# A convolution's closing addition moved, precedence for masks and evacuations, and three later steps in a two-block transformer kernel

## The chip, the cores and the metric

The kernel runs on one core of a Trainium2 chip. The metric is the device time of one execution in microseconds (us). A core has five engines with a queue of their own each: PE (TensorE, the matmuls), DVE (VectorE), ACT (ScalarE), POOL (GpSimd) and SP (SyncE, which here only issues DMAs). An engine works its queue in order, and waits for others by semaphores.

## The reference

512 tokens of 1024 channels pass through two blocks, all in float32. The change concerns the second, which has two layers (0 and 1). Each layer projects the normed input once and gives slices of it to four branches, whose outputs go through one output projection:

```python
def conformer_conv_branch(val, glu_gate, gate, dw_w, dw_b, ln_g, ln_b, pw_w, pw_b):
    h = val * jax.nn.sigmoid(glu_gate)
    h = causal_depthwise_conv(h, dw_w, dw_b)
    h = jax.nn.silu(layer_norm(h, ln_g, ln_b))
...
def hgrn2_branch(q, f_raw, v, gate, lb, norm_g):
    ...
        scores = jnp.einsum('bhtk,bhsk,bhtsk->bhts', qt, kt, decay)
        o_intra = jnp.einsum('bhts,bhsv->bhtv', scores, vt)
...
def mla_branch(cq, ckv, k_rope, gate, positions, qa_g, qb_w, kva_g, kvb_w):
    q = (rms_norm(cq, qa_g) @ qb_w).reshape(bsz, s, D_HEADS, D_NOPE + D_ROPE)
    ...
```

The convolution has 31 taps on 256 channels, hgrn2 works in chunks of 64 tokens, and the fourth branch is a state-space one (ssd). The first block is not touched.

## The kernel before

**Matmuls.** A float32 product is made of three matmuls of parts: high weights by high and by low input, low weights by high input (`mm3`, L466 to L468, 128x512 a piece; L1469, L1470 and L1474 likewise; with tokens on the partitions L1493, L1494 and L1491, 128x256 a piece). Each weight group is loaded by SP (L436, `wr`), copied on ACT to `wh` (L439) and to `wl` = -`wh` (L441), and POOL then issues a DMA that adds the weights to `wl` (L442, 512 KB). So ACT and POOL's DMA queue carry the weights beside all else.

**Tasks.** The program of a layer runs through its projections on PE in order, and after each calls `pump()`, which lets every open task, a Python generator, go on to its next `yield`: `hgrn_task` twice (tasks 0 and 1), `mla_kv`, `mla_q`, `conf_conv`, and so on. The order in which the program writes instructions is their priority; `high_priority(offset=400)` puts what is written inside 400 places ahead. A scheduler then fixes each engine's order from the priorities and from a timeline that it keeps itself. So a `yield` more moves a task's later instructions behind some of the projections, and the order on the engines need not follow the program.

**Buffers.** 70 SBUF tiles of 128 partitions ("units") are given out and taken back as a queue, oldest first. A unit that is given out again makes its writer wait for the last reader, which may be a DMA. PSUM has tags pj (3 buffers), sA (2), sB (2), so (1).

**The convolution** (`conf_conv`, L1505 to L1541). For each of two halves of the channels ("conv 0", "conv 1") the taps 0 to 21 run on DVE into `c` (L1523), a product and an addition in one. The other nine are products on ACT (L1517, L1519 and seven of L1529, named here by their columns, x488 to x482), and POOL adds the seven to two accumulators `e` and `e2` in turn with accumulating DMAs (L1530). One more DMA adds `e2` to `e` (L1534), and DVE adds `e` to `c` (L1539). The task steps by tap pairs (`TAPS` = 2).

**hgrn** (`hgrn_task`, L1772 on). The scores in a chunk come in levels 1, 4, 8, 16, 32: for each, `hgrn_level` makes factors (L1676 to L1685 for level 1; L1695, L1696, L1697, L1705, L1706 for the others, on DVE, POOL and ACT), PE makes the scores (L345 for level 1, L1746 for the others), and `copy_predicated` on DVE puts them through a mask into D (L1766 for level 1, the "finest masks"; L1750 for the others). Behind the levels come three transposes of K2 on PE, their evacuation `kt` on ACT (L1811) and the states' matmuls `pn` (L1817).

**MLA.** `mla_kv` (L2069 on) turns the rotary part of the keys by products and a sum (L2078, L2080), a step later PE transposes them into sB (L2085). `mla_proj` (L2104 on) makes the queries with `mm3` into pj, evacuated on ACT in halves (L2115); the rotary part by DVE (L2124, L2125); the keys likewise (L2134, L2135).

Of the kernel before, what the change touches and what calls it, by code (L numbers as in the profile page):

```python
# [18 lines left out]
S = 512  # L19
# [293 lines left out]
class Build:  # L313
# [1191 lines left out]
    def conf_conv(self, l, ths):  # L1505
        nc = self.nc
        V, G = nc.vector, nc.gpsimd
        for i in range(2):
            while ths[i] is None:
                yield  # L1510
            th, aw = ths[i], self.aw
            c, e = self.unit(F32, "cc"), self.unit(F32, "ce")
            e2 = self.unit(F32, "ce")
            V.tensor_scalar(out=c[:, :S], in0=th[:, :S], scalar1=aw[:, i, 30:31],
                            scalar2=self.v(f"awb{l}", i, i + 1), op0=ALU.mult, op1=ALU.add)
            n0 = 31 - self.POOL_TAPS
            nc.scalar.activation(out=e[:, n0:S], in_=th[:, :S - n0], func=AF.Copy, scale=aw[:, i, 30 - n0:31 - n0])  # L1517
            k = n0 + 1
            nc.scalar.activation(out=e2[:, k:S], in_=th[:, :S - k], func=AF.Copy, scale=aw[:, i, 30 - k:31 - k])  # L1519
            rest = list(range(n0 + 2, 31))  # L1520
            acc = [e, e2]
            for o in range(1, n0):
                V.scalar_tensor_tensor(out=c[:, o:S], in0=th[:, :S - o], scalar=aw[:, i, 30 - o:31 - o], in1=c[:, o:S],  # L1523
                                       op0=ALU.mult, op1=ALU.add)
                if o % self.TAPS == 0:
                    if rest:
                        k = rest.pop(0)
                        t = self.unit()
                        nc.scalar.activation(out=t[:, :S - k], in_=th[:, :S - k], func=AF.Copy, scale=aw[:, i, 30 - k:31 - k])  # L1529
                        nc.gpsimd.dma_start(out=acc[0][:, k:S], in_=t[:, :S - k], accum_op=ALU.add)  # L1530
                        acc.reverse()
                        self.free(t)
                    elif e2 is not None:
                        nc.gpsimd.dma_start(out=e[:, n0 + 1:S], in_=e2[:, n0 + 1:S], accum_op=ALU.add)  # L1534
                        self.free(e2)
                        e2 = None
                    yield
            assert not rest and e2 is None
            V.tensor_tensor(out=c[:, n0:S], in0=c[:, n0:S], in1=e[:, n0:S], op=ALU.add)  # L1539
            self.free(th, e)  # L1540
            self.cs[i] = c  # L1541

    TAPS = 2
    POOL_TAPS = 9
# [193 lines left out]
    def hgrn_score(self, D, X, li, m):  # L1738
# [24 lines left out]
                          rhs=c[sl, w * 128 + 64:w * 128 + 128], start=True, stop=True)  # L1763
        for hh in range(2):
            if m == 1:
                nc.vector.copy_predicated(out=self.v4(D[hh]), mask=self.msk[li].unsqueeze(1).to_broadcast([128, 4, 128]),  # L1766
                                          data=p[hh].rearrange("p (w t) -> p w t", w=4))
            else:
                nc.scalar.activation(out=self.v4(D[hh])[0:64, :, 64:128],
                                     in_=p[hh][:64, :256].rearrange("p (w t) -> p w t", w=4), func=AF.Copy)  # L1770

    def hgrn_task(self, l, i, q_, k_, b_):  # L1772
# [16 lines left out]
        for n in range(5):  # L1789
            if n < 2:  # L1790
                yield
            if n < 3:
                X[LV[n + 2]] = self.hgrn_level(q, k, b, LV[n + 2], Z[(n + 1) % NZ])
            elif n == 3:
                KE, QE, K2, Q2, e = self.hgrn_wide(q, k, b)
                self.free(q_, k_, b_)
            m = LV[n]
            self.hgrn_score(D, X[m], n if n > 1 else 1 - n, m)
            yield
            yield  # L1800
            self.free(X[m][0])
            if m == 1:
                self.free(X[m][1])
# [7 lines left out]
        nc.scalar.activation(out=kt[:, :384], in_=pt[:, :384], func=AF.Copy)  # L1811
        self.hgrn_score(D, (KE, QE), 0, 64)
        self.free(KE, QE, K2)
        yield
        pn = self.sA()
        for w in range(3):
# [252 lines left out]
    def mla_kv(self, l, m):  # L2069
# [10 lines left out]
        V.tensor_tensor(out=kr, in0=kr, in1=t, op=ALU.add)  # L2080
        self.tok_norm(m, 1, 128, 1.0 / 128)
        yield
        pk = self.sB()
        for j in range(4):
            nc.tensor.transpose(pk[:32, j * 128:j * 128 + 128], kr[:, j * 32:j * 32 + 32], self.ident)  # L2085
# [18 lines left out]
    def mla_proj(self, w0, w1):  # L2104
# [6 lines left out]
        for t in range(2):  # L2111
            p = self.pj()
            self.mm3(p, w0[0], w0[1], t * 128, 128, 2, xq, slice(0, S), kstep=256)
            for hh in range(2):
                nc.scalar.activation(out=qs[t * 2 + hh][:64, :S], in_=p[hh * 64:hh * 64 + 64], func=AF.Copy, scale=SC)  # L2115
            self.pump()
        pr = self.pj()
        self.mm3(pr, w1[0], w1[1], 0, 128, 2, xq, slice(0, S))
# [2 lines left out]
        for x in xq:  # L2121
            self.free(*x)
        ro, t = self.unit(), self.unit()
        V.tensor_tensor(out=ro[:, :S], in0=pr, in1=self.cosT, op=ALU.mult)  # L2124
        V.tensor_tensor(out=t[:, :S], in0=px, in1=self.sinT, op=ALU.mult)  # L2125
        G.tensor_tensor(out=ro[:, :S], in0=ro[:, :S], in1=t[:, :S], op=ALU.add)
        for h in range(4):
            nc.scalar.activation(out=qs[h][64:96, :S], in_=ro[h * 32:h * 32 + 32, :S], func=AF.Copy, scale=SC)
# [2 lines left out]
        for t in range(2):  # L2131
            p = self.pj()
            self.mm3(p, w1[0], w1[1], 512 + t * 128, 128, 1, [xk], slice(0, S))
            nc.scalar.activation(out=ks[t * 2][:64, :S], in_=p[0:64], func=AF.Copy)  # L2134
            nc.scalar.activation(out=ks[t * 2 + 1][:64, :S], in_=p[64:128], func=AF.Copy)  # L2135
        self.pump()
        vt = []
        for t in range(2):
# [409 lines left out]
```

## Time and profile before

| what | value |
|---|---|
| three runs | 1370.59, 1372.15, 1372.16 us (median 1372.15) |
| profiled execution, own time | 1370.83 us |
| its span, first to last instruction | 1368.9 us |
| mean granted clock of TensorE | 0.988 |
| busy: PE, DVE, ACT, POOL | 97%, 57%, 57%, 32% of the span |

The page of the profile gives each engine's busy time, the chain of work that ended last (followed back from the last instruction, at each step to what released it), and the costliest groups of instructions. The list of waits says for one engine what it stood still for; the timeline lists its instructions one by one, and the table by stretch gives busy times and the granted clock (1.00 is 2.4 GHz, 0.5 is 1.2 GHz). The instructions whose order the change alters run from about 813 us to the end, those of layer 1 from about 1090 us.

### The profile page before, as it was taken

What the parts mean: (1) busy time and instruction counts of PE and PEld (TensorE: products, weight loads), DVE (VectorE), ACT (ScalarE), POOL (GpSimd) and SP (SyncE); (2) the same over time, 40 slices, a digit from 0 to 9 for tenths busy, and PEclk for the clock granted to TensorE, in tenths of its full rate; (3) what the DMA queues carried; (4) which work ended last, traced back from release to release, by engine and by line L of the source; (5) the groups of instructions that cost most, each with busy time, mean ns of one, the idle gap of its engine ahead of it and who ended that gap; (6) DMA issues with size and microseconds to landing.
All of it is one profiled execution on the core that took longest, in us unless ns stands there. A gap on an engine that the chain in (4) does not pass through costs nothing.

```text
span 1368.9 us, 22975 instructions
## 1 busy us (share of the span) xinstructions
PE 1329.9 (97%) x8778; PEld 1195.9 (87%) x8778; DVE 783.2 (57%) x1961; ACT 782.3 (57%) x1218; POOL 439.1 (32%) x547
## 2 busy tenths in 40 slices
PE   8999999999999999999999999899999889999997
PEld 8888899999999988998898788788988888789986
DVE  8989775423524321332233395798732797987623
ACT  7656564754555443444444775675556876764653
POOL 4557632113332221221123462332211453422210
PEclk9999999999999999999999999999999999999999
DMA  8945566598888889888887975796467676893573
GB/s 269 253 96 109 121 127 138 123 222 186 187 189 186 189 186 188 189 186 190 189 180 150 220 164 131 149 203 136 100 133 166 133 170 138 181 211 81 119 151 92
DMA packets 76861, 223.49 MB, mean 163 GB/s; under 512 B 11216, under 2 KB 21968, under 8 KB 76752
## 3 DMA queue, kind: packets, MB, share of 16 engines
q0 software_dynamic: 32256, 106.53, 47.3%
q1 hardware_dynamic: 43488, 113.80, 25.2%
q8 instruction: 69, 1.13, 0.4%
q10 hardware_dynamic: 1008, 1.70, 0.3%
q14 instruction: 40, 0.33, 0.1%
HBM read 209.33 MB, written 4.72 MB: 156 GB/s over the span
## 4 chain that ended last, share of the span: by engine, by line
PE 77%; DVE 11%; DMA 5%; ACT 3%; issue 3%; POOL 1%; SPq 0%; DVEq 0%; POOLq 0%; ACTq 0%
PE pj L466 14%; PE pj L468 14%; PE pj L467 14%; PE pj L1469 3%; PE pj L1470 3%; PE pj L1474 3%; PE pj L1493 2%; PE pj L1494 2%; PE pj L1491 2%; PE sB L493 2%; DMA ce<-u 2%; DMA wl<-in_wst 2%; PE sB L2167 1%; PE so L2195 1%; DVE hZ L1705 1%
## 5 line engine op out<-in xcount | busy, mean ns | idle before, releaser
L466 PE MATMUL pj<-xh,wh 128*128 128x512 f32 (+4 forms) x1468 | 463.7, 316 | 6.5 <-ACT mq L2115 4.7
L467 PE MATMUL pj<-xl,wh 128*128 128x512 f32 (+4 forms) x1468 | 461.4, 314 | 0.0
L468 PE MATMUL pj<-xh,wl 128*128 128x512 f32 (+4 forms) x1468 | 460.7, 314 | 0.1
L439 ACT ACTIVATE wh<-wr 128x1024 fp32r<-128x1024 f32 (+2 forms) x197 | 204.0, 1036 | 325.0 <-PE pj L467 258.0
L442 POOL DMA_DIRECT2D wl<-in_wst x192 | 170.5, 888 | 568.7 <-ACT wl L441 540.6
L466 PEld LDWEIGHTS pj<-xh,wh 128*128 128x128 f32 x1468 | 278.1, 190 | 25.3 <-ACT mq L2115 4.8
L467 PEld LDWEIGHTS pj<-xl,wh 128*128 128x128 f32 x1468 | 278.1, 189 | 18.3 <-issue 0.6
L468 PEld LDWEIGHTS pj<-xh,wl 128*128 128x128 f32 x1468 | 278.1, 189 | 18.1 <-DMA wl<-in_wst 0.6
L441 ACT ACTIVATE wl<-wh 128x1024 fp32r<-128x1024 f32 (+2 forms) x192 | 198.9, 1036 | 16.4 <-PE pj L1474 8.9
L1494 PE MATMUL pj<-wh,xl 128*128 128x256 f32 x384 | 98.4, 292 | 0.0
L1493 PE MATMUL pj<-wh,xh 128*128 128x256 f32 x384 | 98.0, 291 | 0.0
L1469 PE MATMUL pj<-xh,wh 128*128 128x512 f32 x232 | 93.0, 401 | 0.0
L1470 PE MATMUL pj<-xl,wh 128*128 128x512 f32 x232 | 92.5, 399 | 0.0
L1493 PEld LDWEIGHTS pj<-wh,xh 128*128 128x128 f32 x384 | 74.1, 193 | 1.3 <-issue 1.0
L1494 PEld LDWEIGHTS pj<-wh,xl 128*128 128x128 f32 x384 | 74.3, 194 | 0.8 <-issue 0.5
L1407 DVE TENSOR_TENSOR hT<-hT,pj 128x512 f32<-128x512 f32 x24 | 16.4, 687 | 88.8 <-PE pj L468 88.8
L1523 DVE SCALAR_TENSOR_TENSOR cc<-u,aw,cc 128x511 f32<-128x511 f32 (+17 forms) x84 | 65.8, 786 | 0.6
L1474 PE MATMUL pj<-xh,wl 128*128 128x512 f32 x232 | 62.2, 400 | 0.0
L1386 DVE TENSOR_TENSOR u<-pj,nsR 128x258 f32<-128x258 f32 (+1 forms) x44 | 18.6, 425 | 75.6 <-PE pj L468 68.3
L1491 PE MATMUL pj<-wl,xh 128*128 128x256 f32 x384 | 57.1, 290 | 0.0
L1392 DVE TENSOR_TENSOR u<-u,pj 128x512 f32<-128x512 f32 x22 | 15.1, 687 | 64.6 <-PE pj L468 60.3
L1469 PEld LDWEIGHTS pj<-xh,wh 128*128 128x128 f32 x232 | 43.6, 188 | 9.3 <-issue 0.5
(636 smaller groups left out, 2550.9 us busy)
## 6 DMA issues: line engine op xcount, KB each, us to landing
wr<-in_wst SPq DMA_DIRECT2D x183, 512.0 KB, 4.1
wl<-in_wst POOLq DMA_DIRECT2D x180, 512.0 KB, 5.9
hT<-in_xT SPq DMA_DIRECT2D x16, 264.0 KB, 4.8
wr<-in_wst SPq DMA_DIRECT2D x8, 384.0 KB, 3.1
wl<-in_wst POOLq DMA_DIRECT2D x8, 384.0 KB, 5.7
wr<-in_wst SPq DMA_DIRECT2D x6, 256.0 KB, 2.7
UD<-us SPq DMA_DIRECT2D x4, 264.0 KB, 7.4
U<-UD SPq DMA_DIRECT2D x16, 66.0 KB, 5.0
```

Of the source, the lines that this page charges most:

```text
L439: nc.scalar.activation(out=h[:, c], in_=raw[:, c], func=AF.Copy)
L441: nc.scalar.activation(out=l[:, c], in_=h.bitcast(F32)[:, c], func=AF.Copy, scale=-1.0)
L442: nc.gpsimd.dma_start(out=l[:, c], in_=self.ap["wst"][i, :, c], accum_op=ALU.add)
L466: mm(out=out, lhsT=a, rhs=xh[:, sl], start=k == 0, stop=False)
L467: mm(out=out, lhsT=a, rhs=xl[:, sl], start=False, stop=False)
L468: mm(out=out, lhsT=b, rhs=xh[:, sl], start=False, stop=k == nk - 1)
L1469: mm(out=p, lhsT=a, rhs=xh[:, :S], start=k == 0, stop=False)
L1470: mm(out=p, lhsT=a, rhs=xl[:, :S], start=False, stop=False)
L1474: mm(out=p, lhsT=wl[:, k * 128:k * 128 + 128], rhs=xh[:, :S], start=False, stop=k == 7)
L1491: mm(out=o, lhsT=xh[:, sl], rhs=ws[q][1][:, c], start=False, stop=q + u + k == 5)
L1493: mm(out=o, lhsT=xh[:, sl], rhs=ws[q][0][:, c], start=q + u + k == 0, stop=False)
L1494: mm(out=o, lhsT=xl[:, sl], rhs=ws[q][0][:, c], start=False, stop=False)
```

## The change

Three things, all in the second block:

1. `conf_conv`: the closing addition of `e` to `c` gets a function, `close`; that of conv 0 is made at the third tap pair of conv 1, that of conv 1 two steps after its last. The DMA that adds `e2` to `e` is issued at the tenth tap pair in place of the eighth.
2. `high_priority(offset=400)` around the finest masks and around MLA's evacuations (queries, rotary products, keys).
3. One `yield` more ahead of three places: in layer 1 before the first hgrn level that the loop makes, before `pn`, and before the transposes in `mla_kv`.

```diff
@@ -1505,6 +1505,13 @@
     def conf_conv(self, l, ths):
         nc = self.nc
         V, G = nc.vector, nc.gpsimd
+        last = None
+
+        def close(i, c, e, n0):
+            V.tensor_tensor(out=c[:, n0:S], in0=c[:, n0:S], in1=e[:, n0:S], op=ALU.add)
+            self.free(e)
+            self.cs[i] = c
+
         for i in range(2):
             while ths[i] is None:
                 yield
@@ -1530,15 +1537,20 @@
                         nc.gpsimd.dma_start(out=acc[0][:, k:S], in_=t[:, :S - k], accum_op=ALU.add)
                         acc.reverse()
                         self.free(t)
-                    elif e2 is not None:
+                    elif o + self.TAPS >= n0:
                         nc.gpsimd.dma_start(out=e[:, n0 + 1:S], in_=e2[:, n0 + 1:S], accum_op=ALU.add)
                         self.free(e2)
                         e2 = None
+                    if last and o >= 3 * self.TAPS:
+                        close(*last)
+                        last = None
                     yield
             assert not rest and e2 is None
-            V.tensor_tensor(out=c[:, n0:S], in0=c[:, n0:S], in1=e[:, n0:S], op=ALU.add)
-            self.free(th, e)
-            self.cs[i] = c
+            self.free(th)
+            last = (i, c, e, n0)
+        yield
+        yield
+        close(*last)
 
     TAPS = 2
     POOL_TAPS = 9
@@ -1763,8 +1775,9 @@
                           rhs=c[sl, w * 128 + 64:w * 128 + 128], start=True, stop=True)
         for hh in range(2):
             if m == 1:
-                nc.vector.copy_predicated(out=self.v4(D[hh]), mask=self.msk[li].unsqueeze(1).to_broadcast([128, 4, 128]),
-                                          data=p[hh].rearrange("p (w t) -> p w t", w=4))
+                with self.tc.high_priority(offset=400):
+                    nc.vector.copy_predicated(out=self.v4(D[hh]), mask=self.msk[li].unsqueeze(1).to_broadcast([128, 4, 128]),
+                                              data=p[hh].rearrange("p (w t) -> p w t", w=4))
             else:
                 nc.scalar.activation(out=self.v4(D[hh])[0:64, :, 64:128],
                                      in_=p[hh][:64, :256].rearrange("p (w t) -> p w t", w=4), func=AF.Copy)
@@ -1788,6 +1801,8 @@
             G.memset(t[:, :S], 0.0)
         for n in range(5):
             if n < 2:
+                yield
+            if l and n == 0:
                 yield
             if n < 3:
                 X[LV[n + 2]] = self.hgrn_level(q, k, b, LV[n + 2], Z[(n + 1) % NZ])
@@ -1811,6 +1826,7 @@
         nc.scalar.activation(out=kt[:, :384], in_=pt[:, :384], func=AF.Copy)
         self.hgrn_score(D, (KE, QE), 0, 64)
         self.free(KE, QE, K2)
+        yield
         yield
         pn = self.sA()
         for w in range(3):
@@ -2080,6 +2096,7 @@
         V.tensor_tensor(out=kr, in0=kr, in1=t, op=ALU.add)
         self.tok_norm(m, 1, 128, 1.0 / 128)
         yield
+        yield
         pk = self.sB()
         for j in range(4):
             nc.tensor.transpose(pk[:32, j * 128:j * 128 + 128], kr[:, j * 32:j * 32 + 32], self.ident)
@@ -2112,7 +2129,8 @@
             p = self.pj()
             self.mm3(p, w0[0], w0[1], t * 128, 128, 2, xq, slice(0, S), kstep=256)
             for hh in range(2):
-                nc.scalar.activation(out=qs[t * 2 + hh][:64, :S], in_=p[hh * 64:hh * 64 + 64], func=AF.Copy, scale=SC)
+                with self.tc.high_priority(offset=400):
+                    nc.scalar.activation(out=qs[t * 2 + hh][:64, :S], in_=p[hh * 64:hh * 64 + 64], func=AF.Copy, scale=SC)
             self.pump()
         pr = self.pj()
         self.mm3(pr, w1[0], w1[1], 0, 128, 2, xq, slice(0, S))
@@ -2121,8 +2139,9 @@
         for x in xq:
             self.free(*x)
         ro, t = self.unit(), self.unit()
-        V.tensor_tensor(out=ro[:, :S], in0=pr, in1=self.cosT, op=ALU.mult)
-        V.tensor_tensor(out=t[:, :S], in0=px, in1=self.sinT, op=ALU.mult)
+        with self.tc.high_priority(offset=400):
+            V.tensor_tensor(out=ro[:, :S], in0=pr, in1=self.cosT, op=ALU.mult)
+            V.tensor_tensor(out=t[:, :S], in0=px, in1=self.sinT, op=ALU.mult)
         G.tensor_tensor(out=ro[:, :S], in0=ro[:, :S], in1=t[:, :S], op=ALU.add)
         for h in range(4):
             nc.scalar.activation(out=qs[h][64:96, :S], in_=ro[h * 32:h * 32 + 32, :S], func=AF.Copy, scale=SC)
@@ -2131,8 +2150,9 @@
         for t in range(2):
             p = self.pj()
             self.mm3(p, w1[0], w1[1], 512 + t * 128, 128, 1, [xk], slice(0, S))
-            nc.scalar.activation(out=ks[t * 2][:64, :S], in_=p[0:64], func=AF.Copy)
-            nc.scalar.activation(out=ks[t * 2 + 1][:64, :S], in_=p[64:128], func=AF.Copy)
+            with self.tc.high_priority(offset=400):
+                nc.scalar.activation(out=ks[t * 2][:64, :S], in_=p[0:64], func=AF.Copy)
+                nc.scalar.activation(out=ks[t * 2 + 1][:64, :S], in_=p[64:128], func=AF.Copy)
         self.pump()
         vt = []
         for t in range(2):
```

Nothing is added or left out: every engine has as many instructions as before, and SP's order is the same. Line numbers grow by 7 to 20 (L1529 is L1536 after the change, L1685 is L1697, L1746 is L1758, L1766 is L1779, L1811 is L1826, L1890 to L1900 are L1906 to L1916, L2115 is L2133). Three places follow; out<-in are the program's tiles.

DVE in layer 0, the rows that end with the finest masks (L1766, hD<-msk,sB) of hgrn task 0, before (L509 to L519 and L1896 to L1901 are small steps on vectors of the norms and of ssd):

```order
L515 TENSOR_SCALAR s_8748<-s_8745 128x4
L517 TENSOR_TENSOR s_8747<-s_8746 128x4
L518 TENSOR_TENSOR s_8747<-s_8747,s_8748 128x4
L519 SCALAR_TENSOR_TENSOR s_8746<-s_8747,s_8746 128x4
L1685 TENSOR_TENSOR u_9076<-u_9076,u_8499 128x512
L517 TENSOR_TENSOR s_8747<-s_8746 128x4
L1898 RECIPROCAL s_8705<-s_8705 128x16
L1766 COPY_PREDICATED hD_8600<-msk,sB_8780 128x512
L1766 COPY_PREDICATED hD_8599<-msk,sB_8779 128x512
```

and now:

```order
L518 TENSOR_TENSOR s_8747<-s_8747,s_8748 128x4
L519 SCALAR_TENSOR_TENSOR s_8746<-s_8747,s_8746 128x4
L517 TENSOR_TENSOR s_8747<-s_8746 128x4
L1914 RECIPROCAL s_8705<-s_8705 128x16
L518 TENSOR_TENSOR s_8747<-s_8747,s_8748 128x4
L1915 TENSOR_TENSOR s_8704<-s_8704,s_8705 128x16
L519 SCALAR_TENSOR_TENSOR s_8746<-s_8747,s_8746 128x4
L1697 TENSOR_TENSOR u_9076<-u_9076,u_8499 128x512
L1916 TENSOR_TENSOR s_8706<-s_8706,s_8704 128x16
L517 TENSOR_TENSOR s_8747<-s_8746 128x4
L1779 COPY_PREDICATED hD_8600<-msk,sB_8780 128x512
L1779 COPY_PREDICATED hD_8599<-msk,sB_8779 128x512
```

The addition of 512 columns (L1685, now L1697) still comes ahead of the masks; five small steps more do. Further up, one level's subtraction (L1695) and one pair of products (L1705, for task 1's level 8) have left, to come later.

ACT in layer 0, at the beginning of conv 1's products (u<-u,aw and ce<-u,aw) and the first queries' evacuation (mq<-pj), before:

```order
L1517 ACTIVATE ce_9596<-u_9341,aw_8419 128x490
L1519 ACTIVATE ce_9597<-u_9341,aw_8419 128x489
L1529 ACTIVATE u_9603<-u_9341,aw_8419 128x488
L1529 ACTIVATE u_9706<-u_9341,aw_8419 128x486
L2115 ACTIVATE mq_9444<-pj_9448 64x512
L2115 ACTIVATE mq_9445<-pj_9448 64x512
```

and now:

```order
L1524 ACTIVATE ce_9595<-u_9341,aw_8419 128x490
L1536 ACTIVATE u_9602<-u_9341,aw_8419 128x488
L1526 ACTIVATE ce_9596<-u_9341,aw_8419 128x489
L1536 ACTIVATE u_9705<-u_9341,aw_8419 128x486
L2133 ACTIVATE mq_9444<-pj_9448 64x512
L2133 ACTIVATE mq_9445<-pj_9448 64x512
```

The evacuation keeps its place behind x488 and x486, and ce's second product (489) stands between these. On POOL, where conv 0's last DMAs were issued in the order 484, 483, weights, 482, merge, they are now in the order 484, weights, 483, 482, merge.

ACT in layer 1, the rows up to the evacuation of the K2 transposes (L1811, now L1826, u<-sA), before:

```order
L2115 ACTIVATE mq_12699<-pj_12714 64x512
L1517 ACTIVATE ce_12848<-u_12593,aw_11671 128x490
L1529 ACTIVATE u_12855<-u_12593,aw_11671 128x488
L441 ACTIVATE wl_12691<-wh_12690 128x1024
L1811 ACTIVATE u_12777<-sA_12773 128x384
```

and now:

```order
L2133 ACTIVATE mq_12676<-pj_12714 64x512
L441 ACTIVATE wl_12668<-wh_12667 128x1024
L1524 ACTIVATE ce_12835<-u_12557,aw_11671 128x490
L1526 ACTIVATE ce_12836<-u_12557,aw_11671 128x489
L1536 ACTIVATE u_12842<-u_12557,aw_11671 128x488
L1536 ACTIVATE u_12890<-u_12557,aw_11671 128x487
L1826 ACTIVATE u_12796<-sA_12792 128x384
```

The weight step L441 went ahead of conv 1's products, and two products (489, 487) came between 490 and the evacuation. On POOL the order was K copy, 484, Q copy, 483, 482, weights, merge, and is now 484, 483, Q copy, weights, 482, K copy, merge (the K copy, L1733, now L1745, makes half of K2). On PE in layer 1 the transposes L2085 have 56 projection matmuls between them and the first L1746 of the stretch in place of 61; on DVE the product L1680 of level 1 stood ahead of two pairs of L1705 and now stands behind the first, and the addition L1685 has left the rows ahead of L2080.

## Rows read from the trace of the kernel before

**Rows 1.** Page: engines' busy time; shares of the chain that ended last.
```profile
PE 1329.9 (97%) x8778; PEld 1195.9 (87%) x8778; DVE 783.2 (57%) x1961; ACT 782.3 (57%) x1218; POOL 439.1 (32%) x547
...
PE 77%; DVE 11%; DMA 5%; ACT 3%; issue 3%; POOL 1%; SPq 0%; DVEq 0%; POOLq 0%; ACTq 0%
```

**Rows 2.** Waits of PE: what for, us in total, times, longest.
```profile
PE sB L2085 <- DVE hD L1766: 4.9, 1, 4.9
PE pj L466 <- ACT mq L2115: 4.7, 1, 4.7
...
PE sB L1746 <- DVE hZ L1705: 3.1, 1, 3.1
PE sB L2085 <- DVE s L2080: 2.9, 1, 2.9
PE sA L1817 <- ACT u L1811: 2.3, 1, 2.3
```

**Rows 3.** Stretches: us; PE, PEld, DVE, ACT, POOL busy; clock; DMA; GB/s.
```profile
780.00:830.00 50.00, 45.09 (x308) 41.19 (x307) 42.49 (x108) 34.74 (x55) 22.48 (x28) 0.93 0.74 161
...
860.00:890.00 30.00, 25.32 (x142) 21.16 (x141) 24.51 (x54) 18.38 (x28) 11.76 (x15) 0.92 0.79 152
...
1090.00:1130.00 40.00, 34.01 (x256) 32.57 (x255) 37.37 (x100) 29.11 (x49) 19.18 (x22) 0.96 0.77 173
...
1170.00:1190.00 20.00, 17.68 (x108) 14.76 (x108) 19.53 (x45) 14.55 (x23) 7.99 (x11) 0.91 0.97 194
```

**Rows 4.** Chain that ended last, 812 to 832: start, us, what.
```profile
824.01 0.21 PE pj L1494
...
830.03 0.12 PE pj L1494
```

**Rows 5.** DVE timeline, 814 to 824: start, us, line, operation.
```profile
814.87 0.42 DVE L1695 TENSOR_TENSOR hx<-hb 128x256 f32<-128x256 f32 x1
...
817.49 0.84 DVE L1705 TENSOR_TENSOR hZ<-hx,u 64x256 f32<-64x256 f32 x2
818.36 2.05 DVE L1894 TENSOR_SCALAR s<-s 128x16 f32<-128x16 f32 x1
...
820.45 0.17 DVE L1896 TENSOR_SCALAR s<-s 128x16 f32<-128x16 f32 x1
820.53 0.16 DVE L513 TENSOR_SCALAR s<-s 128x4 int32<-128x4 int32 x1
```

**Rows 6.** POOL timeline, 815 to 821.
```profile
818.11 1.35 POOL L1684 TENSOR_TENSOR u<-u,hk 128x512 f32<-128x512 f32 x1 [1.10 <-ACT u L1682]
819.39 0.99 POOL L1788 MEMSET hD<- 128x512 f32 x2
```

**Rows 7.** Chain that ended last, 856 to 890.
```profile
862.59 6.63 DMA ce<-u
...
876.32 7.61 DMA ce<-u
```

**Rows 8.** ACT timeline, 872 to 892; bracketed: the idle time before.
```profile
880.87 0.69 ACT L1519 ACTIVATE ce<-u,aw 128x489 f32<-128x489 f32 x1
883.95 1.29 ACT L1529 ACTIVATE u<-u,aw 128x488 f32<-128x488 f32 x2 [2.39 <-DMA ce<-u]
```

**Rows 9.** POOL timelines, 872 to 888, 1165 to 1190: two weight DMAs.
```profile
874.10 1.22 POOL L442 DMA_DIRECT2D wl<-in_wst  x1
...
1177.76 1.52 POOL L442 DMA_DIRECT2D wl<-in_wst  x1
```

**Rows 10.** Chain that ended last, 1160 to 1190.
```profile
1177.22 5.29 DMA ce<-u
```

**Rows 11.** DVE timeline, 1100 to 1124.
```profile
1106.35 0.81 DVE L1680 TENSOR_TENSOR u<-hb,s 128x512 f32<-128x512 f32 x1
...
1118.29 0.69 DVE L1685 TENSOR_TENSOR u<-u,u 128x512 f32<-128x512 f32 x1
```

**Rows 12.** ACT timeline, 1172 to 1190.
```profile
1183.21 1.04 ACT L441 ACTIVATE wl<-wh 128x1024 fp32r<-128x1024 f32 x1
```

## Prediction

> **What bounds the kernel now.** I read the page first. TensorE (PE) is busy 1329.9 of the 1368.9 us, and 77% of the chain that ended last is PE [rows 1]. The change removes no matmul, so it can only win what PE waits for. I went next to the waits of PE: the reader is to see that five of them, all in the second block, belong to the tiles that the diff touches, and that they add up to 4.9 + 4.7 + 3.1 + 2.9 + 2.3 = 17.9 us [rows 2]. The table by stretch shows where they lie: A, 4.9 us, and B, 4.7 us, in layer 0 (780 to 830 and 860 to 890), C, 3.1 us, and D, 2.9 us, in layer 1 (1090 to 1130), and E, 2.3 us (1170 to 1190) [rows 2, 3]. It also shows a granted clock of 0.91 to 0.96 in these four stretches, so a stall has a tail: after A the steps of the 128x256 matmuls are 0.21 us apart, later 0.12 us [rows 3, 4]. Clock deficit times length gives 3.5, 2.4, 1.6 and 1.8 us for the four, 9.3 in all and partly inside the stalls themselves. Last I read, for each of the five, the chain and the timeline of the engine that ended it, and held the two orders of that engine side by side: that is how far a release really moves.
>
> **The change, part by part.** All its work is moved work: instruction counts of all engines are the same, SP's queue keeps its order, and so every weight load keeps its place on SP.
>
> A: PE's L2085 waits for the finest masks, L1766, on DVE. The precedence doesn't lift them over the small steps ahead of them; in the new order they stand behind the same 128x512 addition as before (L1685, now L1697) and three rows further down. What goes from ahead of them, because the extra yields push one hgrn level back, is one subtraction of 0.42 us and one pair of products, 0.84 us for two [rows 5]; five small steps come in, whose starts lie about 0.1 us apart, as those of L1896 and L513 do [rows 5]. 0.42 + 0.84 - 0.5 = 0.8 us earlier. Below that the bound is 0 (the gone work was hidden behind something else). Above it stands L1894, a 128x16 step that took 2.05 us where its neighbour L1896 took 0.17 [rows 5]; it ran from 818.36 to 820.41, and POOL's L1684 and its two memsets from 818.11 to 820.38 [rows 6]. If that hold did not recur, A would gain another 1.9 us. These three POOL instructions are still there in the new order, one multiply earlier, so I take **-0.8** (bounds 0 and -2.7). The Trainium skill ("SBUF — State Buffer", section "SBUF: two separate sides") says that VectorE and GpSimd share one port pair as an exclusive lock, and that the loser waits for the whole instruction. By that rule no precedence among DVE's own rows can bring L1894's end ahead of POOL's, which speaks against a large gain at A and for -0.8 rather than -2.7; the row agrees.
>
> B: PE's L466 waits for the evacuation L2115 on ACT. In both orders L2115 stands behind the second conv's product x488 (L1529) and x486; the precedence moves nothing there. That product waits for a unit that the last accumulating DMA of conv 0 frees, issued 876.32 and landed 7.61 us later [rows 7]. Two things move. One more product (L1519, 0.69 us, some 0.6 in a row, as the two of L1529 take 1.29 [rows 8]) comes between x488 and L2115: +0.6. On POOL the weight DMA L442, issued 874.10 [rows 9] between conv 0's last two, now stands before both. The nearest prices of that last DMA are 7.61 here, 6.63 for an earlier one [rows 7], 5.29 for its counterpart in layer 1 [rows 10]; I take 6.3, nearer to 6.63 than to 5.29, since the load has a head start but may still be in flight: -1.3. Together **-0.7** (bounds +0.6 and -1.7).
>
> C: PE's L1746 waits for products hZ, L1705, on DVE. L1680 (0.81 us [rows 11], 0.7 of it not overlapped) now stands behind the first pair: **-0.7** (bounds 0 and -0.9). What follows L1680, the sum of L1685, is later by one pair, and it has slack, as D shows next.
>
> D: PE's L2085 of layer 1 waits for L2080, DVE's. L1685 (0.69 [rows 11]) leaves the stretch ahead of it, but the extra yield of mla_kv works against its aim: on PE L2085 now has 56 projection matmuls between it and the first L1746 in place of 61, so PE arrives 5 x 0.12 = 0.6 earlier [rows 4]. **-0.1** (bounds -0.7 and +0.6).
>
> E: PE's L1817 waits for L1811, an evacuation behind conv 1's products on ACT. The second product (some 0.6) now stands ahead of it too, and the weight step L441 (1.04 [rows 12]) has left: -0.4. On POOL, though, a weight DMA now precedes conv 0's last accumulating one, which took 5.29 with that load behind it [rows 9, 10]; in layer 0, with such a load ahead, it took 7.61 [rows 7]. Between +0 and +2.3 I take the middle, +1.1, less the 0.4, rounded: **+0.6** (bounds -0.4 and +1.9). By the Trainium skill ("DMA: Bandwidth & Descriptors", section "Anatomy of one DMA — SWDGE (gpsimd) path") a DMA of GpSimd costs about 2.0 us plus its bytes at 436 GB/s, an estimate of 2.6 us for these 241 KB. By that price the DMA would never be what ends E, and E would be worth -0.4 or better; the rows here, 5.29 to 7.61, differ, and the rows decide.
>
> The other two edits: the closing addition of each conv and the merging DMA change place, the addition by some rows on DVE, the merge from the eighth to the tenth, the last, tap pair. No wait of PE hangs on either [rows 2], so they cost nothing; the cover is the remaining taps of conv 1, and without it the 128x490 addition would cost about what L1685 does, 0.7.
>
> **Sum:** -0.8 - 0.7 - 0.7 - 0.1 + 0.6 = -1.7 us. The tails stay, since each stall shrinks and none goes. Against the profiled execution (1370.83) that is 1369.1. That execution lies 1.3 below the median of the three runs, 1372.15; the four together average 1371.4, so I forecast 1371.4 - 1.7 = **1369.7 us**. The bounds add up to -6.4 and +3.1, so the forecast's own range is 1365.0 to 1374.5. A measurement of this kernel can tell about 0.2%, 2.7 us, from no change: the borders are 1369.4 and 1374.9 about the median.
>
> **Rivals.**
> (1) The waits go as named: masks and evacuations are released early and the yields give the rest time. All five gone would be 17.9 plus up to 9.3 of clock, 1344 to 1353; A and B alone 9.6 plus up to 5.9, 1356 to 1362; one of the two about 6, near 1365. For it: every named wait is on the tile that the diff touches [rows 2]. Against: in the orders neither L1766 nor L2115 passes the rows that held it up, and B and E end on a DMA that no precedence moves [rows 7, 10].
> (2) Slower, in layer 1: the weight load falls between conv 0's last two accumulating DMAs, and each of these, one behind the other, takes the 2.3 us more that separate 7.61 from 5.29; the K copy on POOL stands behind the second's issue and follows. E grows from 2.3 to near 6.5 us and its slow-clock tail with it by about 0.5. From the point at which the last DMA lands over 2.5 us later than now, this outweighs A to D: 1371.4 - 2.3 + 4.6 - 0.4 + 0.5 = 1373.8, and with A to D at nothing 1376.1. For it: two rows that differ by 2.3 with a load ahead and behind [rows 7, 10]. Against: the load is issued with a head start, and may be over.
> (3) The change doesn't do what it says: the order on the waiting engines moves and the releases don't, because DMA landings and POOL's hold set them. 1371 to 1372. For it: B's and E's chains; against: A's and C's work on DVE did move.
>
> **How the numbers follow.** Forecast 0.52, rival 1 0.20, rival 2 0.17, rival 3 0.11. Faster by over 0.2%: all of rival 1 and, as 1369.7 is close to the border, about 0.22 of the forecast: 0.42. Slower: most of rival 2 and the upper end of the forecast, 0.18. The rest, 0.40, is within 0.2%. The range 1362 to 1376 leaves out the large forms of rival 1 (about 0.11) and the worst of rival 2 (about 0.07).
>
> **What would show it.** Right: PE's wait for the finest masks still 3.5 to 4.5 us, that for the query evacuation 3.5 to 5, that for hZ near 2.4, that for the L1811 evacuation 2 to 4.5; clock deficits in the same four stretches. Rival 1: two or more of the five names gone from the list of waits, and PE's idle time under 30 us. Rival 2: L1817's wait (its new line) above 5 us, with the accumulating DMA over 7 us in layer 1. The prediction is wrong in its reading, not only in a size, if a stall over 2 us stands at a tile that the list of before doesn't name.

## The result, and the profile after

The changed kernel takes **1377.53 us** (median of 6 runs, 1374.30 to 1378.75), the kernel before 1370.64 beside it (6 runs, 1368.22 to 1372.16): a ratio of **1.0057** (95% interval 1.0045 to 1.0070; the quotient of the two medians is 1.0050), 7 to 8 us slower. The forecast was 1369.7 in a range of 1362 to 1376. The profiled executions have spans of 1376.9 and 1368.9 us, 8.0 apart, about 1 more than the medians.

The page of the changed kernel, busy times:

```profile
PE 1333.9 (97%) x8778; PEld 1199.3 (87%) x8778; DVE 790.5 (57%) x1961; ACT 780.2 (57%) x1218; POOL 438.5 (32%) x547
```

PE has the same 8778 matmuls. It is busy 4.0 us longer than in [rows 1], and idle about 4 us longer: slower steps and more waiting come in equal parts. What PE waited for (us in total, times, longest):

```profile
PE sB L1758 <- DVE hZ L1717: 5.3, 1, 5.3
PE pj L466 <- ACT mq L2133: 4.0, 1, 4.0
PE pj L2165 <- ACT mk L2155: 3.6, 1, 3.6
PE sA L1833 <- ACT u L1826: 3.3, 1, 3.3
...
PE sB L2102 <- DVE hD L1779: 2.8, 1, 2.8
PE sB L493 <- ACT mw L2204: 2.6, 2, 1.3
```

Line numbers are the changed kernel's: L2102 is the transposes of L2085, L1758 is L1746, L1833 is L1817, L2133 the query evacuation, L2155 a key evacuation. Against [rows 2], A fell from 4.9 to 2.8, B from 4.7 to 4.0, D (2.9) is gone, C rose from 3.1 to 5.3 and E from 2.3 to 3.3: the five together fell from 17.9 to 15.4. But two tiles stand there that [rows 2] doesn't have: the key evacuation mk, 3.6, and the attention weights mw, 2.6 in two waits (0.3 in the whole list of before). The stretches of the changed kernel show where the clock was low (columns as in [rows 3]):

```profile
780.00:830.00 50.00, 47.16 (x314) 43.07 (x313) 40.87 (x107) 34.93 (x55) 21.40 (x27) 0.93 0.74 163
...
860.00:890.00 30.00, 26.03 (x145) 21.75 (x145) 26.33 (x55) 16.80 (x25) 11.67 (x15) 0.94 0.84 162
890.00:920.00 30.00, 26.39 (x141) 21.41 (x140) 23.77 (x52) 22.88 (x38) 9.59 (x11) 0.94 0.85 186
...
1090.00:1130.00 40.00, 34.67 (x266) 33.92 (x265) 34.10 (x88) 30.52 (x47) 16.52 (x21) 0.91 0.75 172
...
1170.00:1190.00 20.00, 17.61 (x113) 14.74 (x111) 19.85 (x39) 11.50 (x17) 7.91 (x12) 0.99 0.86 176
1190.00:1240.00 50.00, 49.13 (x253) 40.61 (x254) 44.48 (x104) 33.03 (x57) 16.04 (x19) 0.93 0.91 192
```

and two of the kernel before that [rows 3] doesn't hold:

```profile
890.00:920.00 30.00, 30.00 (x160) 24.55 (x159) 27.60 (x62) 23.56 (x39) 10.96 (x12) 0.97 0.89 197
...
1190.00:1240.00 50.00, 50.00 (x287) 42.21 (x282) 43.35 (x106) 32.35 (x56) 14.80 (x16) 1.00 0.86 183
```

The new wait lies in 890 to 920: PE busy 26.39 us in place of 30.00, at 0.94 in place of 0.97. The slow stretch behind E, which lay in 1170 to 1190 before (0.91), comes later and lies in 1190 to 1240 (0.93 in place of 1.00). Clock deficit times length, as the prediction reckoned it, is 3.5 + 1.8 + 1.8 + 3.6 + 0.2 + 3.5 = 14.4 here; before it was 9.3 [rows 3] and 0.9 in 890 to 920.

How the new wait comes about is read from ACT's timeline in layer 0 (start, us, line, operation, in brackets the idle time before):

```profile
882.34 0.70 ACT L1536 ACTIVATE u<-u,aw 128x488 f32<-128x488 f32 x1 [0.43 <-DMA ce<-u]
...
887.52 0.49 ACT L1826 ACTIVATE u<-sA 128x384 f32<-128x384 f32 x1
892.08 0.70 ACT L1536 ACTIVATE u<-u,aw 128x484 f32<-128x484 f32 x1 [4.07 <-DMA ce<-u]
892.68 1.04 ACT L441 ACTIVATE wl<-wh 128x1024 fp32r<-128x1024 f32 x1
...
894.22 0.59 ACT L2155 ACTIVATE mk<-pj 64x512 f32<-64x512 f32 x1
```

and from the chain that ended last:

```profile
874.12 8.20 DMA ce<-u
...
883.92 8.07 DMA ce<-u
...
892.08 0.19 ACT u L1536
...
894.22 0.60 ACT mk L2155
...
894.86 0.39 PE pj L2165
```

ACT is free from 888.0, and PE stands from 891.3 (894.86 less 3.6). Ahead of the key evacuations in ACT's queue stands conv 1's product x484, and this waits 4.07 us for an accumulating DMA that was issued at 883.92 and took 8.07. That DMA is the one of x488, of the same conv: x484 is to be written into the unit that x488 has only just given back. The built programs show which unit a tile lies in. Before, x484 got the unit that conv 0's accumulator `e` had given back a moment earlier, and in the queue of free units the one of x488 came right behind it. In the change `e` comes back only at conv 1's third tap pair, when x488's unit is already in the queue; it stands behind that one instead of ahead of it, everybody in between moves up by one, and x484 gets x488's. Its place on ACT changed too: before, x484 ran at 905.99, behind the keys, and the product ahead of them was x487, which waited for nothing.

### The profile page after: what moved, and what is told of

Its sections match the earlier page's. It is cut to its first block, busy times and chain, and to the rows that moved or that the text cites. A ratio compares the mean times of both kernels' runs of the same rounds, so it can differ in the third digit from the quotient of the medians.

```text
span 1376.9 us, 22975 instructions
## 1 busy us (share of the span) xinstructions
PE 1333.9 (97%) x8778; PEld 1199.3 (87%) x8778; DVE 790.5 (57%) x1961; ACT 780.2 (57%) x1218; POOL 438.5 (32%) x547
## 4 chain that ended last, share of the span: by engine, by line
PE 75%; DVE 11%; DMA 5%; ACT 4%; issue 3%; POOL 1%; SPq 0%; DVEq 0%; POOLq 0%; ACTq 0%
PE pj L466 14%; PE pj L467 14%; PE pj L468 14%; DMA ce<-u 3%; PE pj L1469 3%; PE pj L1470 3%; PE pj L1474 3%; PE pj L1493 2%; PE pj L1494 2%; PE pj L1491 2%; PE sB L493 2%; PE so L2215 1%; PE sB L2187 1%; PE pj L2379 1%; PE pj L2380 1%
## 5 line engine op out<-in xcount | busy, mean ns | idle before, releaser
L441 ACT ACTIVATE wl<-wh 128x1024 fp32r<-128x1024 f32 (+2 forms) x192 | 198.8, 1035 | 22.5 <-PE pj L1474 5.2
```

The lines of the kernel that those rows point to most:

```text
L441: nc.scalar.activation(out=l[:, c], in_=h.bitcast(F32)[:, c], func=AF.Copy, scale=-1.0)
```

## The experiments

Three theories stood at the outset. **Theory 1:** late closing withholds a unit, and conv 1's products get units whose DMAs are in flight. **Theory 2:** the extra steps cost the time. **Theory 3:** only both together do. Each ratio below is to the kernel before, run beside it on the same chip; 6 runs of it stand beside the changed kernel, and 29, 32 and 35 beside the three groups of experiments.

| kernel | ratio | 95% interval | median, us |
|---|---|---|---|
| changed kernel | 1.0057 | 1.0045 to 1.0070 | 1377.53 |
| conv_only | 1.0058 | 1.0039 to 1.0077 | 1377.69 |
| yields_only | 0.9987 | 0.9972 to 1.0002 | 1368.42 |
| after_late_close | 1.0031 | 1.0015 to 1.0046 | 1374.12 |
| after_late_merge | 1.0007 | 0.9994 to 1.0021 | 1371.27 |
| after_other_unit | 0.9994 | 0.9979 to 1.0010 | 1369.99 |
| pn_layer0 | 0.9984 | 0.9967 to 1.0000 | 1367.41 |
| hold_units | 1.0068 | 1.0044 to 1.0091 | 1379.30 |
| hold_units_pn0 | 0.9983 | 0.9967 to 1.0000 | 1368.38 |
| precedence_only | 1.0011 | 0.9997 to 1.0025 | 1371.19 |
| hold_units_sum_on_dve | 1.0026 | 1.0011 to 1.0042 | 1373.00 |
| hold_units_sum_on_dve_pn0 | 1.0027 | 1.0007 to 1.0047 | 1372.50 |
| hold_units_late_close | 0.9968 | 0.9944 to 0.9992 | 1364.24 |

**The parts alone.** conv_only is the kernel before with the whole first edit:

```diff
+        last = None
+        def close(i, c, e, n0):
...
-                    elif e2 is not None:
+                    elif o + self.TAPS >= n0:
...
-            V.tensor_tensor(out=c[:, n0:S], in0=c[:, n0:S], in1=e[:, n0:S], op=ALU.add)
+            last = (i, c, e, n0)
```

> The kernel before with the convolution's edit alone (closing addition and merging DMA later). Theory 1 (late closing keeps conv 0's accumulator unit out of the free queue, so a product of conv 1 that stands ahead of the key evacuations on ACT gets the unit of x488, whose accumulating DMA is still in flight): a new PE wait of 3 to 4 us for a key evacuation near 895 us in layer 0, one or two waits of about 1.3 us for mw, and 4 to 8 us more than before. Theory 2 (the extra steps cost the time, the convolution is innocent): within 2 us of before, no wait for a key evacuation. Theory 3 (only both together cost it): within 2 us of before.

Measured 1.0058: the convolution's edit alone is as slow as the whole change. PE's waits:

```profile
PE sB L1758 <- DVE hZ L1717: 5.4, 1, 5.4
PE sB L2097 <- DVE hD L1778: 4.9, 1, 4.9
PE pj L466 <- ACT mq L2127: 4.8, 1, 4.8
...
PE sB L493 <- ACT mw L2196: 2.6, 2, 1.6
PE pj L2157 <- ACT mk L2147: 2.2, 2, 1.4
```

The key evacuation (L2157 <- mk) and mw are there, the first smaller than expected, 1.4 us near 895 and 0.8 in layer 1. So the whole loss comes with less of that wait than in the changed kernel: the wait alone is not its measure. A and B, 4.9 and 4.8, are those of before; the rise of C to 5.4 comes from this edit too.

yields_only has the three extra `yield`s and nothing else:

```diff
+            if l and n == 0:
+                yield
...
         self.free(KE, QE, K2)
         yield
+        yield
...
         self.tok_norm(m, 1, 128, 1.0 / 128)
         yield
+        yield
```

> The kernel before with the three extra steps alone. Theory 1: no PE wait for a key evacuation; the wait for the finest masks near 2.8 us in place of 4.9, and 0 to 4 us less than before. Theory 2: 4 to 8 us more than before, with the wait for hZ near 5.3 and that for the L1811 evacuation near 3.3. Theory 3: within 2 us of before.

Measured 0.9987, so theory 2 falls, and with conv_only theory 3. PE's waits:

```profile
PE sB L2089 <- DVE s L2083: 4.7, 1, 4.7
...
PE sA L1820 <- ACT u L1813: 4.0, 1, 4.0
...
PE sB L2089 <- DVE hD L1766: 2.9, 1, 2.9
...
PE sB L1746 <- DVE hZ L1705: 1.8, 1, 1.8
```

No key evacuation. The extra steps take A to 2.9 and C to 1.8, and they lengthen two of the waits that they were put ahead of: D goes from 2.9 to 4.7 and E from 2.3 to 4.0.

precedence_only has the `high_priority` lines alone:

```diff
+                with self.tc.high_priority(offset=400):
+                    nc.vector.copy_predicated(out=self.v4(D[hh]), ...)
```

> The kernel before with the precedence alone. The orders of all five engines are word for word those of before, and so are the buffers. Theory (precedence moves nothing): the same five waits of PE within 0.5 us each, and the time of before within 2 us. Rival (precedence acts on something that the orders don't show): over 3 us from before.

Every engine's order and every buffer is that of before, with the precedence and without it; and the changed kernel built without the precedence is the same program as with it. The five waits A to E are 4.7, 5.6, 3.2, 2.8 and 2.4, B further from its 4.7 than was expected, and the ratio 1.0011 (0.9997 to 1.0025) is what one and the same program shows against itself: a ratio within 0.2% of 1 says nothing here. So yields_only, pn_layer0 and hold_units_pn0 are not shown to be faster than before. The DMAs differ as well: the last accumulating DMA of conv 0 in layer 0, which took 7.61 us from 876.32 in the trace of before [rows 7], took 4.38 here:

```profile
881.26 4.38 DMA ce<-u
```

**Which half of the convolution's edit.** after_late_close is the changed kernel with the merge back at the eighth pair, after_late_merge with the closing additions back at the end of each conv:

```diff
-                    elif o + self.TAPS >= n0:
+                    elif e2 is not None:
```

> The changed kernel with the merging DMA back at the eighth tap pair; the closing addition stays late. Theory 1: the key evacuation's wait of 3 to 4 us stays, and the time is that of the changed kernel within 3 us, 4 to 8 us more than before. Theory 2: like the changed kernel too. Rival to theory 1 (the late merge is what does it): the wait goes, and the time falls to that of before or under.

> The changed kernel with each closing addition back at the end of its conv; the merging DMA stays at the tenth tap pair. Theory 1: no wait for a key evacuation, time 0 to 4 us under before, as with the extra steps alone. Theory 2: 4 to 8 us more than before. Rival (late merge): the wait of 3 to 4 us stays and 4 to 8 us more than before.

With late closing alone (beside the extra steps) the key evacuation's wait stays (2.6 us, under the 3 to 4 expected), B is 6.6, and the ratio is 1.0031; with the late merge alone the key evacuation's wait goes, and the ratio is 1.0007, where 0 to 4 us under before had been expected. From 0.9987 without either, late closing adds some 6 us, the late merge some 3, and both over 9. The 3 of the merge are within what precedence_only shows, and remain open.

**The unit alone.** after_other_unit is the changed kernel where one product takes another unit:

```diff
+                        if l == 0 and i == 1 and k == 28:
+                            self.free_units.insert(0, self.free_units.pop(5))
                         t = self.unit()
```

> The changed kernel, where in layer 0 the product x484 of conv 1 takes the sixth of the free units instead of the first, which is x488's own. Theory 1 (that unit is what holds the key evacuation): the wait of 3.6 us for the key evacuation near 895 us goes, the time falls by 3 to 6 us from the changed kernel's, to 2 to 4 us over before; the waits for mw (1.3 each) stay. Rival (the accumulating DMA or the late closing holds ACT in any unit): the wait stays and the time is that of the changed kernel.

```profile
PE pj L466 <- ACT mq L2135: 4.7, 1, 4.7
...
PE sB L1760 <- DVE hZ L1719: 2.4, 1, 2.4
...
PE sA L1835 <- ACT u L1828: 1.6, 1, 1.6
...
PE sB L493 <- ACT mw L2206: 1.3, 1, 1.3
```

The key evacuation's wait is gone, and 0.9994 in place of 1.0057 is more than was expected: all of the loss. ACT's timeline shows the keys evacuated as soon as PE has made them:

```profile
886.54 1.05 ACT L441 ACTIVATE wl<-wh 128x1024 fp32r<-128x1024 f32 x1
888.25 0.59 ACT L2156 ACTIVATE mk<-pj 64x512 f32<-64x512 f32 x1 [0.66 <-PE pj L468]
```

More went than that wait, because the scheduler then orders the rest of the second block anew (C 2.4 in place of 5.3, E 1.6 in place of 3.3, one wait for mw in place of two), x484 itself first: with the other unit it runs at 903.87, behind the keys. In the three kernels in which it lies in x488's unit it runs ahead of them, at 892.08 (the changed kernel), 892.90 (conv_only) and 892.39 (after_late_close). So the unit and the place on ACT come together, and the experiment doesn't part them.

Where the loss arises is seen at a matmul of the norm between the two layers, in the changed kernel and with the other unit:

```profile
1073.72 0.77 PE L2439 MATMUL sB<-nsA,o 128*128 128x256 f32 x1 [2.81 <-DVE nsA L532]
```
```profile
1067.03 0.45 PE L2441 MATMUL sB<-nsA,o 128*128 128x256 f32 x1 [2.80 <-DVE nsA L532]
```

Of the 10.2 us between the two profiled spans (1376.9 and 1366.7), 6.7 have arisen by then, in layer 0, and 3.5 follow in layer 1. So handing x484 that unit is shown to be the cause of the whole loss here, and the 3.6 us to be its first step; how much of the rest is that wait and its slow clock, and how much is the new order, is not shown, nor that it would follow in another program.

**One step alone.** pn_layer0 has, of the three steps, the one ahead of `pn`, in layer 0:

```diff
         yield
+        if not l:
+            yield
         pn = self.sA()
```

> The kernel before with one extra step alone: the one ahead of pn, in layer 0 only. Theory 1 (this step is what shortened the wait for the finest masks, and in layer 1 the same step lengthened the wait for the L1811 evacuation): wait for the masks near 2.9 in place of 4.9, layer 1's waits as before (hZ 3.1, L2080 2.9, L1811 2.3), 1 to 3 us less than before. Rival (the gain of the three steps came from layer 1): masks' wait 4.9, time within 1 us of before.

Measured 0.9984. The masks' wait is 2.9: A's gain comes from this step. Layer 1 didn't stay as it was, against the expectation: of its three waits only hZ, 3.1, is there, and a key evacuation of 1.8 has come, as later units change there too.

**Taking the cause away.** hold_units leaves the kernel before as it is, but for the units read by accumulating DMAs, which come back five such DMAs later:

```diff
+    def hold(self, t, n):
+        self.held.append(t)
+        while len(self.held) > n:
+            self.free(self.held.pop(0))
...
-                        self.free(t)
+                        self.hold(t, 5)
...
-                        self.free(e2)
+                        self.hold(e2, 5)
...
+        self.free(*self.held)
+        self.held = []
```

> The kernel before, where the five units last read by an accumulating or merging DMA are kept out of the free queue until the next such, so that a product of conv 1 never gets a unit whose DMA is in flight. Theory 1: PE's waits for the query evacuation (4.7) and for the L1811 evacuation (2.3) go, as do their slow-clock tails: 6 to 12 us less than before. Rival (the DMA chain itself sets these waits, whatever the unit): both waits stay within 1 us, and the time is within 2 us of before.

> The same holding of units with the extra step ahead of pn in layer 0. Theory 1: the gains add: masks' wait near 2.9, no wait for the query or L1811 evacuations, 8 to 14 us less than before. Rival: no better than the extra step alone, 1 to 3 us less than before.

The waits for the query and the L1811 evacuations are gone, as theory 1 has it, and the kernel is 9.6 us slower. The trace is that of its fastest execution, 1373.70 us, 4.0 over the median of before, so it shows less than half of this loss. The waits went elsewhere:

```profile
PE so L2203 <- DVE yd L2210: 9.8, 2, 6.0
...
PE sB L2175 <- ACT hD L1777: 1.8, 1, 1.8
```

DVE's timeline, at the first wait for yd (L2210):

```profile
935.97 0.67 DVE L1545 TENSOR_TENSOR cc<-cc,ce 128x490 f32<-128x490 f32 x1 [10.52 <-DMA ce<-ce]
...
937.12 0.42 DVE L2210 TENSOR_TENSOR yd<-so,s 128x256 f32<-128x256 f32 x1
```

DVE stands 10.52 us at the closing addition (here L1545), which waits for the merging DMA, and yd, which PE waits for, is queued behind it. The other, 1.8, ends on POOL: the sum of the queries' rotary halves stands there behind the merging DMA, which waits 9.1 us for a landing. With the step in layer 0 the same kernel is at 0.9983, no better than the step alone, as the rival has it, with 3.4 and 1.6 us of waits in the attention.

The last three put that sum on DVE, then add the step, then the convolution's edit:

```diff
-        G.tensor_tensor(out=ro[:, :S], in0=ro[:, :S], in1=t[:, :S], op=ALU.add)
+        V.tensor_tensor(out=ro[:, :S], in0=ro[:, :S], in1=t[:, :S], op=ALU.add)
```

> The kernel before with units held as in hold_units, and the sum of the queries' rotary halves on DVE in place of POOL. Theory (holding the units freed ACT, and the wait moved to POOL, where this sum stands behind the merging DMA that waits 9 us for a landing): the PE wait of 1.8 us near 893 us shrinks below 0.5; DVE's closing addition behind the merge still holds yd and the two waits of 6.0 and 3.8 us for yd stay, so 0 to 5 us better than hold_units and not better than before by over 3 us. Rival (holding costs by itself, more late units everywhere): as hold_units, 8 to 11 us over before.

> The same with the extra step ahead of pn in layer 0. Theory: the masks' wait near 2.8 in place of 4.3 to 4.9, no wait over 1 us between 870 and 900 us, 3 to 7 us less than before. Rival: no better than hold_units_pn0, 0 to 3 us less than before.

> The same once more with the convolution's edit (late closing addition and late merge). Theory (late closing is harmful only by the unit that it withholds, and its aim, DVE not waiting for the merge, is right): no wait for a key evacuation, no wait for yd over 2 us, 3 to 9 us less than before. Rival (late closing delays the rest of the convolution branch into the attention whatever the units): waits of 1 us and more for mw near 985 and 1285 us, and a time at or over that of before.

On DVE the sum costs PE no wait near 893, and hold_units falls by 6.3 us to 1373.0; of the two waits for yd that were expected to stay, one of 2.9 is left, and one of 4.6 for sD, on POOL, has come. With the step it should have been 3 to 7 us under before and is at 1.0027: a miss. Its profiled execution took 1364.86 us and its median is 1372.5, so the profile doesn't show where most of its executions lose the time; that is open. hold_units_late_close, which differs from it by the convolution's edit, is the fastest of all, 0.9968 (0.9944 to 0.9992), 5.4 us under the median of before and by the ratios some 12 under the change; its executions lie between 1357.82 and 1373.61 us, further apart than those of any other kernel here:

```profile
PE sB L1766 <- DVE hZ L1725: 3.2, 1, 3.2
...
PE sB L2107 <- DVE s L2102: 2.9, 1, 2.9
PE sB L2107 <- DVE hD L1786: 2.8, 1, 2.8
PE sB L499 <- ACT u L2194: 2.3, 3, 1.5
```

B, E, the key evacuation and yd are gone; C and D are those of before. In this kernel, where units come back late anyway, late closing brings no wait for a key evacuation and no loss. Why it is the fastest is not shown. The theory was that DVE no longer waits for the merge, and it does still, at two closing additions (here L1517):

```profile
929.85 0.67 DVE L1517 TENSOR_TENSOR cc<-cc,ce 128x490 f32<-128x490 f32 x1 [3.16 <-DMA ce<-ce]
...
1187.61 0.67 DVE L1517 TENSOR_TENSOR cc<-cc,ce 128x490 f32<-128x490 f32 x1 [4.98 <-DMA ce<-ce]
```

These are 8.1 us, where DVE in hold_units_sum_on_dve_pn0 waits 7.5 for the merge in one piece (ahead of the closing additions it idles 4.8 and 9.4 us more, for which the profile names no releaser); PE waits for yd in neither. In the kernel before, DVE doesn't wait at the closing addition at all.

## Why the prediction was wrong, point by point

**The step that failed** is the one on the other two edits: "No wait of PE hangs on either [rows 2], so they cost nothing; the cover is the remaining taps of conv 1". I asked when the addition is done and who waits for its result, and not what it gives back: it is also the last reader of `e`, and so the place where a unit returns to a queue in which everyone behind moves up. The order of ACT, in which x484 comes ahead of the keys in the change, had been there to be read, and so had its unit; I followed the products only as far as x486, though B itself rests on such a wait for a unit, that of x488. By the runs this step is worth about +9 us (yields_only to the changed kernel), against nothing in the sum. The five terms of the sum did not make the miss: together they were forecast at -1.7 and measured 17.9 to 15.4, -2.5, though by luck in part, as the single terms show.

**A**, forecast -0.8, measured 4.9 to 2.8. The mechanism was right: other work left DVE's queue, and the hold by POOL stayed but was shorter, 1.23 us where L1894 had taken 2.05 [rows 5, 6], which adds 0.8 to the forecast's 0.8; the rest of the 2.1 is not traced:

```profile
818.21 1.23 DVE L517 TENSOR_TENSOR s<-s 128x4 f32<-128x4 f32 x1
```

**B**, -0.7: 4.7 to 4.0. The size was met, its make-up not: the DMA before it took 8.20 us where I took 6.3, and gained its time by an earlier issue, 874.12 for 876.32 [rows 7]; where two unlike terms gave a sum that fits, that is luck. And 0.7 us is less than one and the same program shows: in precedence_only's trace B is 5.6, and that DMA is issued at 881.26 and takes 4.38. A single trace was no price for it.

**C**, -0.7, was wrong in sign: 3.1 to 5.3. L1680 did move behind the first pair of L1705 (now L1717). But this pair, which PE waits for, took 3.61 us, where it had taken 1.69 (and the next pair 3.09), while POOL worked beside it:

```profile
1113.51 3.61 DVE L1717 TENSOR_TENSOR hZ<-hx,u 64x256 f32<-64x256 f32 x2
```
```profile
1112.45 1.11 POOL L1708 TENSOR_TENSOR hx<-hb 128x256 f32<-128x256 f32 x1 [2.11 <-DVE hb L1678]
...
1114.12 1.01 POOL L1718 TENSOR_TENSOR hx<-hx,hk 128x256 f32<-128x256 f32 x1
1114.79 0.68 POOL L1747 COPY Q<-QE 128x256 f32<-128x256 f32 x1
1115.15 1.68 POOL L1718 TENSOR_TENSOR hx<-hx,hk 128x256 f32<-128x256 f32 x2
```

The 1.9 us between 3.61 and 1.69 are most of the rise of 2.2 in C. I had counted DVE's rows ahead of the pair, as I had at A, but not asked which POOL instructions would lie beside it. The rise belongs to the step that failed: with the extra steps alone C is 1.8, with the convolution's edit alone 5.4. By the Trainium skill ("SBUF — State Buffer", section "SBUF: two separate sides") a VectorE operation with two SBUF inputs and one of GpSimd that reads SBUF exclude each other; the rows agree: 3.61 is 2.8 more than the 0.84 or so of a pair left alone ([rows 5], L1705), and POOL's rows from 1114.12 on last 2.7. **D**, -0.1, is gone with it, since PE came to it later; C and D together, -0.8 by the sum, measured 6.0 to 5.3, which is luck, as each was wrong by over 2.5 us.

**E**, +0.6 with +1.9 as its bound: 2.3 to 3.3, and the clock deficit from 1170 to 1240 grew from 1.8 to 3.7 us. The accumulating DMA behind the weight load took 9.05 us where I had bounded it by 7.61 [rows 7]:

```profile
1179.93 9.05 DMA ce<-u
```

yields_only, where E is 4.0, and conv_only, where it is gone, show that it comes from the extra steps. The estimate of 2.6 us by the Trainium skill ("DMA: Bandwidth & Descriptors", section "Anatomy of one DMA — SWDGE (gpsimd) path") is farther off still from 8.07 and 9.05 (the shortest accumulating DMA in the same chain, 3.19, comes nearest to it); the measurements decide.

**The precedence** does nothing: I said so for L1766 and L2115, and precedence_only shows it for all. **The tails stay** held for A (3.5) and nearly for B (2.4 to 1.8); those of C and E doubled (1.6 to 3.6, 1.8 to 3.7), and the stretch of the new wait for the keys has 1.8 in place of 0.9.

**The rivals.** Rival 2 had the right side, and a place in layer 1 in which a load lengthened a DMA; it gave E 6.5 where 3.3 was measured, and its time, 1373.8 to 1376.1, came out near by luck, since the loss arose in another way. What I had named as proof of a wrong reading, a stall over 2 us at a tile that [rows 2] doesn't name, is what happened. I had the chance of a slower kernel at 0.18, and had priced no case in which a buffer comes free later.

## What to carry to other kernels

Where buffers go round in a queue, a later last reader is a cost of its own: follow not only who waits for the result of a moved instruction, but which buffer it gives back, who gets the next one instead, and what transfer still reads that. An instruction that waits for a buffer in the queue of an engine that also serves PE can make PE wait, however little its own result matters. The duration of a DMA in a single trace is no price: look at a second execution of the same program first. And a scheduler's precedence is worth looking up in the orders before it is given a price: here it changed none.

## What the runs showed of the hardware that was not expected

An accumulating DMA of 241 to 244 KB, issued with a 512 KB weight load near it, took 8.07, 8.20 and 9.05 us in the changed kernel, against 5.29 to 7.61 in the rows of before. The spread within one kernel is as large: other accumulating DMAs in the chain of the changed kernel took 3.19 to 4.29 us, and in two traces of one and the same program, before and precedence_only, the same DMA took 7.61 and 4.38. And that program, built with and without the precedence, measured 0.11% apart.
